# Computing the second layer's modulation beside the first routing stretch instead of beside the first mixer, in 1024-column blocks

## The chip, the cores and the metric

One NeuronCore of one Trainium2 chip runs the whole program in a single launch. The metric is device microseconds of one execution. Times shown are single executions and the median of three.

## The reference, cut to what matters

One inference step of a backbone with two layers, for 128 context tokens (the prompt) and 512 latent tokens (the sample), width 1024. Each layer has a modulated norm, a mixer (attention and retention in layer 0, differential and windowed attention in layer 1), a second modulated norm and a channel mixer that picks, for each token and each of 8 heads, 16 out of 16384 single-neuron experts.

```python
for layer in range(DEPTH):                      # DEPTH = 2
    mod_p = jnp.split(jax.nn.silu(c_ctx)[None, :] @ mod_w[layer] + mod_b[layer], 6, axis=-1)
    mod_s = jnp.split(jax.nn.silu(c) @ mod_w[layer] + mod_b[layer], 6, axis=-1)
    hp = ada(xp, norm_mix[layer], mod_p[0], mod_p[1])
    hs = ada(xs, norm_mix[layer], mod_s[0], mod_s[1])
    ...                                         # mixers: out_p, out_s
    xp = xp + mod_p[2][:, None, :] * out_p
    xs = xs + mod_s[2][:, None, :] * out_s
    xp = xp + mod_p[5][:, None, :] * peer(ada(xp, norm_ffn[layer], mod_p[3], mod_p[4]), ...)
    xs = xs + mod_s[5][:, None, :] * peer(ada(xs, norm_ffn[layer], mod_s[3], mod_s[4]), ...)
```

The modulation of a layer depends only on `c`, `c_ctx` and the weights `mod_w[layer]` (1024 x 6144 floats, 25.2 MB). It doesn't depend on the tokens, so layer 1's can be computed at any time before layer 1's first norm.

## The kernel before

The program has three stretches for each layer, one after the other, each with its own PSUM banks and SBUF pool.

- **M0, M1 (mixer).** The sample's mixer is the main work: input projections, attention, retention, output projection. PSUM: two banks `mm`, two double banks `S`, one `tr`, one `acc`. In M0 the first layer's modulation (`mod`, lines 325 to 358) runs first, at the same time as the first projections.
- **W0, W1 (routing).** `route` projects the queries of the channel mixer (`peer_q`, 16 steps, each loads a 512 KB weight block, splits it into a high and a low part with ScalarE and VectorE, L467 and L468, and multiplies, L478), finds each token's top experts (`pairs`), and then builds gate matrices (`gate_build`): VectorE makes one-hot rows, TensorE multiplies them into banks `gb` (L1403, L1404), ScalarE copies these to a tile `gst` (L1407) that goes to DRAM (`Gd`). Beside it run `dense_pre`, the first half of the dense expert product (`a_block`: load a 512 KB block `u`, split it with L1422 on ScalarE and L1423 on VectorE, 24 matmuls on L1434, a result `gpre` that goes to DRAM as `Ad`), and the gather. PSUM: three banks `mm`, four `gb`.
- **D0, D1 (dense).** The second half of the dense expert product. The prompt's mixer of layer 1, which needs layer 1's modulation, starts in D0.

The gather (`gather_tile`) fetches rows of expert weights by index, 128 x 1024 floats each: GpSimd issues an indirect DMA (L1323), VectorE multiplies (L1336) or accumulates (L1340). It runs through M0 to D1.

The order of the work is written out by generators. A `Task` steps a generator; `weave(main, *tasks)` steps the main one and gives every other task the main task's step cost times its rate as credit. Each engine executes its instructions in the order that results, and so does the DMA queue of SyncE (SP), on which all weight loads stand: a load that waits for a free tile holds up every load behind it.

The second layer's modulation is `mod_strips(1)` (from L361), a side task of M0 with rate `M1R` = 0.4. It goes over 12 strips of 512 columns. For each strip it takes an `mm` bank, loads eight 256 KB tiles `mw` (L371) through a ring of three (`MWB`), and for each tile does four matmuls (L373), one for each group of 32 PE columns; float32 operands make each of these two records in the trace. ScalarE copies the bank to `modsb` (L376), TensorE transposes it (L322) into an `mm` bank, and VectorE adds the bias (L381). 12 strips of 8 tiles are 96 tile steps.

In W0 the weight blocks of `peer_q` and the `u` blocks share one ring of three SBUF tiles, `w32` (`bufs=self.wb`, L461 and L1415): the load of a block waits until the block three before it has been split.

## Time and profile before

| | |
|---|---|
| median of 3 runs | 4050.77 us (4027.24 to 4058.07) |
| the profiled execution | 4050.72 us |
| its span, first to last instruction | 4048.9 us |
| outside the span | 1.8 us |
| M0, as far as the matmuls of `mod_strips` reach into it | 141.6 to 625.7 us |
| start of the chain's wait for the first `peer_q` block, in W0 | 716.95 us |
| first matmul of D0 | 1310.9 us |

Engines in the rows: PE is TensorE (PEld its weight loads), DVE VectorE, ACT ScalarE, POOL GpSimd, SP SyncE. "L373 PE MATMUL mm<-mw,c_silu" is line 373, a matmul that writes tile `mm` from `mw` and `c_silu`. In a wait, "A <- B: 15.3, 6, 5.8" says that A waited for B 15.3 us in all, 6 times, 5.8 us at the longest. The chain is the sequence of work that ended last, followed backwards from the last instruction; its shares are of the stretch named.

### The profile page before, as it was taken

The numbers are of one execution on the slowest core, as the hardware profiler recorded it, in microseconds if no ns is written. First come the engines' busy times: TensorE is split into PE (matmuls) and PEld (weight loads), VectorE is DVE, ScalarE is ACT, GpSimd is POOL, SyncE is SP. The second block draws the span as 40 slices with busy tenths as digits, with TensorE's granted clock in tenths as the row PEclk, the third lists the DMA queues.
The fourth block names the chain that finished last, engine by engine and source line by source line (L and its number), as shares of the span: only waits on it lengthen the run. The fifth ranks groups of instructions, "written<-read, shape, count | busy, mean of one in ns | idle before, by whom it ended". The sixth has DMA issues, their size and how long they took to land.

```text
span 4048.9 us, 57028 instructions
## 1 busy us (share of the span) xinstructions
PE 3653.0 (90%) x19986; PEld 3060.2 (76%) x19986; DVE 3180.2 (79%) x6370; ACT 1620.7 (40%) x2971; POOL 1621.2 (40%) x1138
## 2 busy tenths in 40 slices
PE   7888889889997999999998898988976999999998
PEld 3675556778886877888886676777875888888887
DVE  3238668999997767778897898899997667777777
ACT  3222223334776433433333333333476634333333
POOL 1004445320554234443464676532075233444342
PEclk9999989999998999999999999999997999999999
DMA  8556778775798889899896777777577889999886
GB/s 320 179 176 235 276 281 281 252 233 181 277 363 323 308 294 358 301 338 347 303 351 250 241 244 231 257 257 232 188 266 274 331 301 333 345 337 324 301 309 213
DMA packets 441087, 1134.86 MB, mean 280 GB/s; under 512 B 40640, under 2 KB 191360, under 8 KB 434528
## 3 DMA queue, kind: packets, MB, share of 16 engines
q0 software_dynamic: 147968, 537.36, 37.7%
q1 hardware_dynamic: 251408, 506.28, 36.3%
q10 hardware_dynamic: 41424, 87.57, 5.8%
q8 instruction: 157, 2.57, 0.2%
q14 instruction: 130, 1.06, 0.1%
HBM read 1045.08 MB, written 85.98 MB: 279 GB/s over the span
## 4 chain that ended last, share of the span: by engine, by line
PE 48%; DVE 16%; DMA 8%; issue 8%; ACT 5%; POOL 2%; ACTq 0%; DVEq 0%; POOLq 0%; SPq 0%
PE d L1457 21%; PE mm L1434 14%; PE mm L478 5%; DMA u<-ut 3%; DVE acc L1340 3%; DVE row L1336 2%; DMA row<-u,xi 2%; PE pm L482 2%; DVE ulo L1423 2%; ACT gst L1407 2%; POOL row L1323 1%; DMA Gd<-gst 1%; ACT uhi L1422 1%; PE S L708 1%; DMA Ad<-gpre 1%
## 5 line engine op out<-in xcount | busy, mean ns | idle before, releaser
L1323 POOL DMA_INDIRECT row<-v,xi x512 | 832.3, 1626 | 1114.1 <-DVE acc L1340 773.6
L1323 POOL DMA_INDIRECT row<-u,xi x512 | 681.3, 1331 | 789.0 <-DVE row L1336 585.2
L1434 PE MATMUL mm<-hhi,uhi 128*128 128x384 f32 x2048 | 709.6, 346 | 46.9 <-ACT uhi L1422 43.2
L1434 PE MATMUL mm<-hhi,ulo 128*128 128x384 f32 x2048 | 707.2, 346 | 49.3 <-DVE ulo L1423 49.1
L1434 PE MATMUL mm<-hlo,uhi 128*128 128x384 f32 x2048 | 702.6, 343 | 2.2 <-DVE hlo L452 1.6
L1336 DVE SCALAR_TENSOR_TENSOR row<-hn,row 128x1024 f32<-128x1024 f32 x512 | 630.0, 1257 | 47.4 <-DMA row<-u,xi 39.8
L1340 DVE SCALAR_TENSOR_TENSOR acc<-row,gw,acc 128x1024 f32<-128x1024 f32 x508 | 650.6, 1281 | 4.2 <-DMA row<-v,xi 1.6
L1457 PE MATMUL d<-vlo,Whi 128*128 128x512 f32 x1536 | 482.1, 394 | 5.6 <-DVE vlo L1498 5.6
L1457 PE MATMUL d<-vhi,Wlo 128*128 128x512 f32 x1536 | 479.0, 393 | 0.0
L1422 ACT CAST uhi<-u 128x1024 fp32r<-128x1024 f32 x256 | 268.8, 1050 | 491.8 <-PE mm L1434 226.8
L1423 DVE TENSOR_TENSOR ulo<-u,uhi 128x1024 fp32r<-128x1024 f32 x256 | 313.5, 1225 | 185.0 <-ACT uhi L1422 183.7
L1457 PE MATMUL d<-vhi,Whi 128*128 128x512 f32 x1536 | 437.3, 397 | 16.9 <-ACT vhi L1497 13.2
L1434 PEld LDWEIGHTS mm<-hhi,uhi 128*128 128x128 f32 x2048 | 396.5, 194 | 65.1 <-ACT uhi L1422 54.4
L1434 PEld LDWEIGHTS mm<-hhi,ulo 128*128 128x128 f32 x2048 | 395.3, 193 | 66.0 <-DVE ulo L1423 62.7
L1434 PEld LDWEIGHTS mm<-hlo,uhi 128*128 128x128 f32 x2048 | 395.2, 193 | 8.7 <-DVE hlo L452 2.0
L1457 PEld LDWEIGHTS d<-vhi,Whi 128*128 128x128 f32 x1536 | 288.1, 190 | 74.9 <-ACT vhi L1497 17.3
L1457 PEld LDWEIGHTS d<-vhi,Wlo 128*128 128x128 f32 x1536 | 288.0, 188 | 61.4 <-issue 0.2
L1457 PEld LDWEIGHTS d<-vlo,Whi 128*128 128x128 f32 x1536 | 286.4, 189 | 62.8 <-DVE vlo L1498 8.0
L1498 DVE TENSOR_TENSOR vlo<-v,vhi 128x1024 fp32r<-128x1024 f32 x256 | 312.2, 1221 | 14.2 <-ACT vhi L1497 13.9
L1505 ACT CAST Whi<-W 128x384 fp32r<-128x384 f32 x256 | 131.2, 513 | 433.1 <-PE d L1457 337.1
L1497 ACT CAST vhi<-v 128x1024 fp32r<-128x1024 f32 x256 | 268.5, 1051 | 53.3 <-DMA v<-v 41.9
L478 PE MATMUL mm<-hhi,whi 128*128 128x512 f32 x624 | 255.4, 410 | 31.5 <-DVE rvs L594 12.6
(470 smaller groups left out, 5776.4 us busy)
## 6 DMA issues: line engine op xcount, KB each, us to landing
u<-ut SPq DMA_DIRECT2D x256, 512.0 KB, 5.3
v<-v SPq DMA_DIRECT2D x256, 512.0 KB, 6.2
Gd<-gst ACTq DMA_DIRECT2D x48, 1024.0 KB, 8.7
G<-Gd SPq DMA_DIRECT2D x64, 768.0 KB, 8.8
w<-win SPq DMA_DIRECT2D x80, 512.0 KB, 4.7
w<-wq SPq DMA_DIRECT2D x64, 512.0 KB, 5.2
Ad<-gpre ACTq DMA_DIRECT2D x152, 192.0 KB, 4.5
pre<-Ad SPq DMA_DIRECT2D x152, 192.0 KB, 6.0
```

What stands on the lines that cost most here:

```text
L478: nc.tensor.matmul(ps[:, :st.T], wp[a][:, k], h[b][:, k], start=(n == 0), stop=(n == 23))
L482: nc.tensor.matmul(ps[:, :st.T], w32[:, k], h[:, k], start=(k == 0), stop=(k == 7))
L1323: nc.gpsimd.indirect_dma_start(out=r, out_offset=None, in_=self.A[f"{'uv'[n // 128]}{l}"], in_offset=bass.IndirectOffsetOnAxis(ap=xi[:, s: ...
L1336: nc.vector.scalar_tensor_tensor(r, hn, 1.0, r, op0=ALU.mult, op1=ALU.mult, accum_out=a[:, s:s + 1])
L1340: nc.vector.scalar_tensor_tensor(acc, r, w[:, s:s + 1], acc, op0=ALU.mult, op1=ALU.add)
L1422: nc.scalar.copy(hi, u)
L1423: nc.vector.tensor_tensor(lo, u, hi, op=ALU.subtract)
L1434: nc.tensor.matmul(ps[:, :ND], u[a][:, k], h[b][:, k, :ND], start=n == 0, stop=n == 23)
L1457: nc.tensor.matmul(acc[t][hf], a[:, ts], b[:, hf * 512:(hf + 1) * 512], start=(i == 0 and n == 0), stop=(i == 127 and n == 2))
L1497: nc.scalar.copy(vhi, v)
L1498: nc.vector.tensor_tensor(vlo, v, vhi, op=ALU.subtract)
L1505: nc.scalar.copy(whi, w)
```

## The change

`mod_strips` goes, and `mod_ahead` takes its place: a side task of W0 in layer 0, with rate 0.16. It goes over 6 blocks of 1024 columns; each tile `mw` is 128 x 1024 floats, 512 KB, and comes through the ring `w32`; each of its four matmuls has 256 columns. It has one PSUM bank of its own, `ms`, for the sums and the transposes, and W0 of layer 0 has three banks `gb` instead of four. M0 loses the task, its pool and its ring.

```diff
-M1R = 0.4
+M1R = 0.16
...
-    def mod_strips(self, l):
+    def mod_ahead(self, l):
...
-        for g in range(12):
-            ps = self.bank("mm")
+        for g in range(6):
+            ps = self.bank("ms")
             for k in range(8):
-                w = self.wk.tile([128, 512], F32, tag="mw", name="mw", bufs=MWB)
-                nc.sync.dma_start(w, self.A["mod_w"][l, k * 128:(k + 1) * 128, g * 512:(g + 1) * 512])
+                w = self.wk.tile([128, 1024], F32, tag="w32", name="mw", bufs=self.wb)
+                nc.sync.dma_start(w, self.A["mod_w"][l, k * 128:(k + 1) * 128, g * 1024:(g + 1) * 1024])
                 for j in range(4):
-                    nc.tensor.matmul(ps[32 * j:32 * j + 32, :128], c["silu"][:, k], w[:, j * 128:(j + 1) * 128],
+                    nc.tensor.matmul(ps[32 * j:32 * j + 32, :256], c["silu"][:, k], w[:, j * 256:(j + 1) * 256],
                                      start=(k == 0), stop=(k == 7), tile_position=(0, 32 * j))
-            sb = self.wk.tile([128, 128], F32, tag="sb", name="modsb", bufs=1)
-            nc.scalar.copy(sb, ps[:, :128])
-            yield 6.8
-            pt = self.bank("mm")
-            self.transpose(pt[:, :128], sb)
+                yield 1.0
+            sb = self.wk.tile([128, 256], F32, tag="msb", name="modsb", bufs=1)
+            nc.scalar.copy(sb, ps[:, :256])
+            pt = self.bank("ms")
+            for b in range(2):
+                self.transpose(pt[:, b * 128:(b + 1) * 128], sb[:, b * 128:(b + 1) * 128])
             for s in range(2):
...
-                if l == 0:
-                    weave(sample, prompt, ahead, gath)
-                    ahead.drain()
-                    ma.close()
-                else:
-                    weave(sample, prompt, gath)
+                weave(sample, prompt, gath)
...
-            with self.psum(f"W{l}", mm=W_MM, gb=W_GB), self.sbuf(f"W{l}"):
+            with self.psum(f"W{l}", mm=W_MM, gb=W_GB - 1, ms=1) if l == 0 else self.psum(f"W{l}", mm=W_MM, gb=W_GB), \
+                    self.sbuf(f"W{l}"):
...
                 side = [gath, pre]
+                if l == 0:
+                    side.append(Task(self, self.mod_ahead(1), M1R))
...
                 weave(route, *side, prompt)
```

Three places show what the change does to the order of instructions. Line numbers of the changed kernel differ by one or two. The first is SP's queue of loads in M0, in retention of the first head pair (`win` is the projection weight, `qf` and `qb` ramps). Before:

```order
L799 DMA ramp<-qf 128x512
L462 DMA w_3264<-win 128x1024
L371 DMA mw<-mod_w 128x512 x6
L799 DMA ramp<-qb 128x512
L462 DMA w_3311<-win 128x1024
L371 DMA mw<-mod_w 128x512 x2
L462 DMA w_3824<-win 128x1024
```

Now:

```order
L800 DMA ramp<-qf 128x512
L463 DMA w_2933<-win 128x1024
L800 DMA ramp<-qb 128x512
L463 DMA w_2980<-win 128x1024
L463 DMA w_3383<-win 128x1024
```

The loads of `mod_w` between the mixer's loads are gone, and nothing else in the queue has changed place. The second is the same queue where W0 begins (`wout` is the end of M0, `wq` the weight of `peer_q`, `ut` the blocks `u`). Before:

```order
L462 DMA w_5409<-wout 128x1024
L1416 DMA u_5557<-ut 128x1024
L462 DMA w_5594<-wq 128x1024
L1416 DMA u_5639<-ut 128x1024
L462 DMA w_5672<-wq 128x1024
L462 DMA w_5744<-wq 128x1024
L462 DMA w_5813<-wq 128x1024
L1416 DMA u_5886<-ut 128x1024
```

Now:

```order
L463 DMA w_4740<-wout 128x1024
L1417 DMA u_4887<-ut 128x1024
L370 DMA mw<-mod_w 128x1024 x2
L463 DMA w_4939<-wq 128x1024
L1417 DMA u_4984<-ut 128x1024
L370 DMA mw<-mod_w 128x1024
L463 DMA w_5023<-wq 128x1024
L370 DMA mw<-mod_w 128x1024
L463 DMA w_5101<-wq 128x1024
```

A load of `mod_w` now stands before nearly every load of `wq`, and two stand before the first; 24 of the 48 stand ahead of the first gate matrix, and 24 among the `u` loads of `gate_build`, there after every first or second `u`; the last fifteen `u` loads of W0 follow the last of them. The third is VectorE at a bias addition, before in M0 (a strip late in retention):

```order
L1336 SCALAR_TENSOR_TENSOR row,ga<-hn,row 128x1024
L381 TENSOR_TENSOR mod_854<-mm,c_mod_b 128x4 x2
L1336 SCALAR_TENSOR_TENSOR row,ga<-hn,row 128x1024
L386 SCALAR_TENSOR_TENSOR gs_855<-mod_854,c_gffn 128x8 x2
L819 TENSOR_TENSOR SD<-S,D_4426 128x512
```

and now in W0, in `peer_q` (the first of six):

```order
L1136 MATCH_REPLACE psr<-ptv,psc 128x128
L1138 MAX_INDEX pti<-ptv,psc 128x8
L381 TENSOR_TENSOR mod_4920<-ms,c_mod_b 128x8 x2
L469 TENSOR_TENSOR wlo<-w_5547,whi 128x1024
L1140 MAX ptv<-psr 128x8 x4
L1142 MAX_INDEX pti<-ptv,psr 128x8 x4
```

The two additions, which need a transpose on TensorE, stood among the gather's multiplications and now stand ahead of the split of a `peer_q` weight block and of the search for the top 16.

## Rows read from the trace of the kernel before

**Rows 1.** The page's head and its busy times of the engines.
```profile
span 4048.9 us, 57028 instructions
PE 3653.0 (90%) x19986; PEld 3060.2 (76%) x19986; DVE 3180.2 (79%) x6370; ACT 1620.7 (40%) x2971; POOL 1621.2 (40%) x1138
```

**Rows 2.** Busy time by stretch: start:end, length, engines, clock, DMA share, GB/s.
```profile
20.00:47.00 27.00, 20.41 (x95) 5.11 (x88) 11.30 (x41) 10.09 (x21) 0.00 (x0) 0.81 1.03 401
130.00:660.00 530.00, 463.50 (x3018) 323.69 (x3017) 327.29 (x834) 151.58 (x347) 182.31 (x154) 0.93 0.69 236
717.00:1050.00 333.00, 295.20 (x1585) 267.06 (x1586) 325.63 (x1061) 135.01 (x213) 84.05 (x62) 0.95 0.67 222
1050.00:1310.00 260.00, 219.41 (x1616) 207.66 (x1615) 220.26 (x308) 184.66 (x421) 133.84 (x66) 0.91 0.89 330
```

**Rows 3.** Groups of `mod_strips`, 130 to 660: busy, mean ns, idle before, releasers.
```profile
L373 PE MATMUL mm<-mw,c_silu 128*32 128x128 f32 x768 | 35.3, 288 | 8.8 <-DMA mw<-mod_w 7.9 <-ACT rqs L662 0.4 <-DVE xp L896 0.3
L322 PE MATMUL mm<-c_ident,modsb 128*128 128x128 f32 x12 | 3.8, 320 | 0.8 <-ACT modsb L376 0.8
L381 DVE TENSOR_TENSOR mod<-mm,c_mod_b 128x4 f32<-128x4 f32 x24 | 2.8, 158 | 15.3 <-PE mm L322 15.3
```

**Rows 4.** Busy time by stretch of line 373 alone: PE, PEld, clock, DMA.
```profile
516.00:660.00 144.00, 9.62 (x208) 4.52 (x208) 0.92 0.79 273
```

**Rows 5.** Chain of waits by line, 516 to 660.
```profile
by line: PE S L816 11.2%; PE mm L478 10.6%; issue 10.5%; PE acc L820 10.4%; PE S L708 8.0%; PE acc L781 7.3%; PE tr L756 7.1%; DMA row<-u,xi 4.9%; PE mm L756 4.3%; DVE row L1336 3.2%; PE mm L373 3.1%; PE acc L804 2.4%; PE mm L498 2.2%; POOL
```

**Rows 6.** Timeline, start and length: wide tile steps of layer 0, a narrow one.
```profile
47.89 1.91 PE L339 MATMUL tr<-modw,c_silu 128*32 128x512 f32 x12
...
549.24 0.42 PE L373 MATMUL mm<-mw,c_silu 128*32 128x128 f32 x8
549.60 1.12 PE L816 MATMUL S<-rqs,rks 128*128 128x512 f32 x2
```

**Rows 7.** Waits 130 to 660: line, for whom, us, times, longest.
```profile
DVE mod L381 <- PE mm L322: 15.3, 6, 5.8
...
PE mm L478 <- DVE rvs L594: 12.6, 3, 6.0
```

**Rows 8.** Waits of VectorE, 717 to 1050, the longest two.
```profile
DVE wlo L468 <- ACT whi L467: 3.6, 2, 3.3
DVE ada_t L445 <- PE mm L410: 1.3, 1, 1.3
```

**Rows 9.** Chain in order of time, W0: pieces of one a_block, of DMA.
```profile
716.95 7.10 DMA w<-wq
...
841.31 4.20 PE mm L1434 x24
...
1077.85 11.69 DMA Gd<-gst
1109.52 14.46 DMA Ad<-gpre
```

**Rows 10.** Chain by line, 1050 to 1310.
```profile
by line: PE mm L1434 25.6%; ACT gst L1407 15.4%; DMA Gd<-gst 10.4%; DMA Ad<-gpre 9.8%; issue 7.0%; ACT gjl L1397 5.6%; ACT uhi L1422 5.3%; DVE acc L1340 3.7%; PE gb L1403 2.3%; PE gb L1404 2.1%; ACT gpre L1436 2.0%; PE mm L1243 1.8%; DVE ul
```

**Rows 11.** DMA issues 1050 to 1310: count, KB, median us to landing.
```profile
u<-ut SPq DMA_DIRECT2D x34, 512.0 KB, 6.2
```

**Rows 12.** Splits of a u block, from the page: busy, mean ns, idle before.
```profile
L1422 ACT CAST uhi<-u 128x1024 fp32r<-128x1024 f32 x256 | 268.8, 1050 | 491.8 <-PE mm L1434 226.8
L1423 DVE TENSOR_TENSOR ulo<-u,uhi 128x1024 fp32r<-128x1024 f32 x256 | 313.5, 1225 | 185.0 <-ACT uhi L1422 183.7
```

**Rows 13.** Waits of TensorE for a gb bank: W0 (660 to 1310).
```profile
PE gb L1403 <- ACT gst L1407: 1.6, 4, 0.6
```

**Rows 14.** The same wait in W1 (3000 to 3260), also with four banks.
```profile
PE gb L1403 <- ACT gst L1407: 22.2, 7, 10.4
```

**Rows 15.** Tile d, the sums of the dense stretches: durations, first and last start.
```profile
L1457 PE MATMUL d<-vhi,Whi x1536: 387/389/792, 1310.9 to 4031.6; 128*128 128x512 f32 x192
```

More of the change, by code (lines that the diff above doesn't have):

```diff
@@ L60 @@
 ML = 1
-MWB = 3
 PDR = 0.7
@@ L366, in mod_strips @@
         self.mg[l] = m, gs
-        for g in range(12):
-            ps = self.bank("mm")
+        for g in range(6):
+            ps = self.bank("ms")
             for k in range(8):
-                w = self.wk.tile([128, 512], F32, tag="mw", name="mw", bufs=MWB)
-                nc.sync.dma_start(w, self.A["mod_w"][l, k * 128:(k + 1) * 128, g * 512:(g + 1) * 512])
+                w = self.wk.tile([128, 1024], F32, tag="w32", name="mw", bufs=self.wb)
+                nc.sync.dma_start(w, self.A["mod_w"][l, k * 128:(k + 1) * 128, g * 1024:(g + 1) * 1024])
                 for j in range(4):
-                    nc.tensor.matmul(ps[32 * j:32 * j + 32, :128], c["silu"][:, k], w[:, j * 128:(j + 1) * 128],
+                    nc.tensor.matmul(ps[32 * j:32 * j + 32, :256], c["silu"][:, k], w[:, j * 256:(j + 1) * 256],
                                      start=(k == 0), stop=(k == 7), tile_position=(0, 32 * j))
-            sb = self.wk.tile([128, 128], F32, tag="sb", name="modsb", bufs=1)
-            nc.scalar.copy(sb, ps[:, :128])
-            yield 6.8
-            pt = self.bank("mm")
-            self.transpose(pt[:, :128], sb)
+                yield 1.0
[4 more added lines that the diff above has]
+                self.transpose(pt[:, b * 128:(b + 1) * 128], sb[:, b * 128:(b + 1) * 128])
             for s in range(2):
-                nc.vector.tensor_tensor(m[:, 4 * g:4 * g + 4, s], pt[:, :128].rearrange("p (j r) -> p j r", r=32)[:, :, s],
-                                        c["mod_b"][:, l, 4 * g:4 * g + 4], op=ALU.add)
-            yield 0.5
+                nc.vector.tensor_tensor(
+                    m[:, g * 8:(g + 1) * 8, s].rearrange("p (j b) -> p j b", b=2),
+                    pt[:, :256].rearrange("p (b j r) -> p j b r", b=2, r=32)[:, :, :, s],
+                    c["mod_b"][:, l, g * 8:(g + 1) * 8].rearrange("p (j b) -> p j b", b=2), op=ALU.add)
         for i, (gain, o) in enumerate((("gmix", 8), ("gffn", 32))):
@@ L1640, in run @@
                 if l == 0:
-                    ma, mp = ExitStack(), ExitStack()
-                    pool = ma.enter_context(tc.tile_pool(name="mod1", bufs=1, reuse_waits="tile"))
-                    ahead = Task(self, self.mod_strips(1), M1R)
-                    ahead.ctx = (pool, pool, 6)
+                    mp = ExitStack()
                     pool = mp.enter_context(tc.tile_pool(name="mod0", bufs=1, side="right", reuse_waits="tile"))
```

## The prediction

> **What bounds the kernel now.** I read the page's head first, then busy time by stretch, then the waits and the chain inside the stretches that the change touches. Over the whole span TensorE is busy 90% and VectorE 79% [rows 1], but that mean says nothing on where a tile step costs time, so the stretches come next. In M0, from the first matmul of the strips to the end (130 to 660 us), TensorE is busy 463.50 of 530 us, VectorE 327.29, the DMA engines 0.69 of the time [rows 2]: nothing is full there, TensorE comes nearest. In the first part of W0 (717 to 1050 us, `peer_q` and `pairs`) VectorE is busy 325.63 of 333 us and TensorE 295.20: VectorE is full. Its longest wait there is 3.6 us in all [rows 8]. In the second part (1050 to 1310, `gate_build`) no engine is full, but the DMA engines are busy 0.89 of the time at 330 GB/s [rows 2], and on the chain stand 10.4% waits for `Gd` and 9.8% for `Ad` [rows 10]; single ones are 11.69 and 14.46 us long [rows 9]. So the work leaves a stretch with some room on every engine and enters one that is full on VectorE in its first part and nearly full on DMA in its second. Everything after W0 keeps its order, and I leave D0 to D1 as they are.
>
> **What M0 gives back.** The matmuls of the strips take 35.3 us of TensorE, the transposes 3.8 us, and TensorE waited 7.9 us for the `mw` loads [rows 3]. How much of it was on the path? From 516 to 660 us the chain spends 3.1% of 144 us on L373, which is 4.5 us, while L373 was busy 9.62 us there [rows 4, 5]: 46%. Going by TensorE's busy share in M0, 463.50 / 530, it would be 87%. I take the middle, 67%: 0.67 x (35.3 + 3.8) = 26 us for the work and 0.67 x 7.9 = 5 us for the waits. Three of the old tiles (3 x 0.26 MB) were loaded ahead of the first layer's modulation, where the DMA engines were full at 401 GB/s [rows 2]: 2 us. Sum: 33 us. Lower bound: 0.46 x 35.3 = 16 us. Upper bound: all of it, plus all 15.3 us that VectorE stood at the bias addition behind a transpose with the gather queued behind it [rows 3, 7]: 35.3 + 3.8 + 7.9 + 15.3 + 2 = 64 us. The upper end is not far-fetched, since each strip also held one of the two `mm` banks while its eight tiles came in; TensorE's 12.6 us of waiting for `rvs`, a copy out of an `mm` bank [rows 7], are the kind of wait that may shrink.
>
> **What W0 takes on**: seven terms, and a price that two of them use.
>
> (1) Start. Two 512 KB tiles now stand ahead of the first `wq` block, for which the chain already waits 7.10 us [rows 9]. 1.05 MB at 330 GB/s is 3 us.
>
> (2) A tile step's price. The trace has no 256-column step. A 128-column step (8 records) occupies TensorE 0.36 us, from 549.24 to the next start at 549.60; 512-column records came 12 in 1.91 us, so 8 in 1.27 us [rows 6]. On the straight line between, 256 columns take 0.66 us; the bounds are 0.36 and 1.27. 48 steps are 32 us, which is about what the 96 narrow ones took: TensorE's work is moved, not saved. 24 of the steps fall before 1050 us, 24 behind it. The Trainium skill (TensorEngine Tiling (Array Packing), section Tiling Modes) says that changing the tiling mode drains the engine; if that drain were the whole price, a step would stay at 0.36 us and the 48 would cost 17 us. Rows 6 speak for a price that grows with the columns, so the sum stays with 0.66.
>
> (3) TensorE, 717 to 1050. 24 x 0.66 + 1.9 us of transposes = 18 us, in a stretch with 333 - 295.20 = 38 us of idle TensorE under a full VectorE. I charge a quarter, 4.5 us (bounds 0 and 18). What hides it is VectorE's work; if TensorE gets late with a score matmul, VectorE waits at once.
>
> (4) VectorE at the bias addition. In M0 the twelve strips cost it 15.3 us of standing, 1.3 us for one [rows 3]. Three of the six new additions stand in the part where VectorE is full, ahead of a weight split on which TensorE depends: 3 x 1.3 = 4 us. Bounds 0 and 3 x 5.8 = 17 us, by the longest such wait [rows 7].
>
> (5) The ring. A `u` or `wq` block whose slot was last held by an `mw` tile can only be requested when TensorE has done that tile's matmuls, where before it was requested when VectorE had split the block three earlier. From request to use it then takes 6.2 us of loading [rows 11] and 1.05 + 1.23 us of splitting [rows 12], 8.5 us. Between lie one or two blocks of 24 matmuls at 4.20 us [rows 9] and, in `gate_build`, the gate matmuls; the 34 `u` loads of 260 us [rows 11] make 7.6 us to a block. With two blocks between, nothing is late; with one, about 1 us, in some 10 places, and half as much again in `peer_q`: 5 us. Bounds 0 and 25.
>
> (6) TensorE, 1050 to 1310. 24 x 0.66 + 1.9 = 18 us. TensorE is busy 219.41 of 260 us [rows 2] but stands on only a third of the chain (25.6 + 2.3 + 2.1 + 1.8% [rows 10]). I take half, 9 us (bounds 6 and 18).
>
> (7) DMA, 1050 to 1310. 24 x 0.524 MB = 12.6 MB. If the engines were full they would need 38 us more at 330 GB/s. The stretch moves 86 MB, so the load rises by 15%, and the 20.2% of the chain that are DMA waits [rows 10], 53 us, would rise to match by 8 us if waits grew only as the bytes do. At a share of 0.89 they grow faster: 15 us, bounds 0 and 38. On this the Trainium skill (DMA: Bandwidth & Descriptors, section Specifications) is harsher: it gives about 358 GB/s as one core's limit from HBM, and by it 12.6 MB in a stretch that runs near it are 35 us. The trace shows 401 GB/s from 20 to 47 us [rows 2], so I don't take that figure as a wall.
>
> (8) The fourth `gb` bank. In W0 TensorE waited 1.6 us for ScalarE to empty one [rows 13]; in W1, the same code with the same four banks, 22.2 us [rows 14]. So the margin is thin. With three: 8 us, bounds 0 and 22. Behind a gate matmul that waits stand the 24 matmuls of the next a_block, and behind these the DMA of `Ad`.
>
> Sum of W0: 3 + 4.5 + 4 + 5 + 9 + 15 + 8 = 48.5 us. Net: 48.5 - 33 = +15.5 us on the execution's own 4050.7 us (span 4048.9 and 1.8 outside), 4066 us. That execution equals the median of the runs shown, so nothing is corrected. The prompt's mixer of layer 1 starts in D0 and finds its modulation finished, since the last `mw` load stands before the last 15 `u` loads of W0.
>
> **Rivals.**
>
> A. M0 was held up by the strips more than by their matmuls: the blocked `mm` bank and the VectorE waits go as well, and M0 returns 64 us. W0 hides nearly all: 3 us of start, 6 of TensorE, 8 of DMA, 3 of the rest, 20 us. Net -44 us: 4007 us. For it: the 15.3 us on VectorE and the gather bursts behind them. Against it: the chain holds only 46% of the strips' matmuls, so other waits lie close beneath.
>
> B. A wash. As forecast, but the ring and the bank cost nothing and the DMA waits grow only as the bytes do: 48.5 - 5 - 8 - 7 = 28.5 against 33 us, 4046 us. For it: 1.6 us of bank waits in W0. Against it: the same wait in W1.
>
> C. Slower, through DMA in `gate_build`: `Gd`, `Ad`, the gather and the `u` loads already fill 0.89 of the engines; the new tiles come on top in full, ScalarE stands longer at `gst`, three banks fill sooner, and `u` loads land late so that the ring's lateness counts. It decides where the share passes about 0.97 for the whole stretch. 38 (DMA) + 22 (banks) + 15 (ring) + 18 (TensorE) + 11.5 (start, terms 3 and 4) = 104 us, less 33: +71 us, 4122 us. The skill's figure on HBM would have it so. For it: 20.2% of the chain; against it: VectorE's and ScalarE's share of the same chain, under which some of it hides.
>
> That the change doesn't do what it says is out: the order of the instructions shows the loads gone from M0 and all 48 in W0.
>
> **How the numbers follow.** The forecast, with errors of its own of about 25 us either way, gets 0.45, B 0.20, C 0.20, A 0.15. A measurement of this kernel can tell about 1%, 40.5 us, from no change: the bounds are 4010 and 4091 us. Faster by over 1%: 0.12 from A and 0.01 from B, 0.13. Slower: 0.20 from C and 0.10 from the forecast's upper end, 0.30. Within 1%: 0.57. The range has to take in most of C and A's edge: 4010 to 4118 us. The likeliest case's own range is 4041 to 4091.
>
> **What would show it.** M0 should end 16 to 64 us earlier: the wait for the first `peer_q` block, now at 716.95 us, should begin near 684. From there to the first matmul of D0, now at 1310.9 [rows 15], was 594 us and should be about 642. In 717 to 1050 VectorE should stay above 95% with new waits of a few us at the bias additions; in `gate_build` the waits for `Gd` and `Ad` should grow and waits of L1403 for `gst` appear. The D stretches and M1, W1 should keep their length within 10 us. The forecast is wrong if W0 grows by less than 30 us (towards A or B) or more than 75 (C), or if the difference lies behind W0 at all.

## The result and the profile after

The changed kernel takes 4025.0 us (median of 19 runs, 4014.5 to 4033.8), the kernel before on the same chips 4049.7 us (19 runs, 4027.2 to 4065.4). The ratio is 0.9943 with a 95% interval of 0.9931 to 0.9955: 0.57% faster, 24.7 us, where 15.5 us slower was forecast. That is less than the 1% that the prediction took for the least difference one can tell, but it is clear, and its sign is the other one.

The head of the page after, beside [rows 1]:

```profile
span 4020.8 us, 56136 instructions
PE 3640.4 (91%) x19602; PEld 3033.4 (75%) x19602; DVE 3182.0 (79%) x6358; ACT 1618.8 (40%) x2965; POOL 1588.2 (40%) x1138
```

The stage ends below are read off the first starts of certain instructions, in us. M0 ends with the first matmul that spreads the sample's norm in W0. The first part of W0 ends at the first copy to `gst`, the gate part at the first matmul of `d`, and so on. The second line is a repeat of the kernel before.

```
                 M0 ends  W0 first  W0 gate  W0 sum  d starts   D0    M1    W1    D1    end
before             717.9     290.4    302.6   593.0    1310.9  890.0 441.3 624.9 781.8 4048.9
before, again      707.2     291.0    303.0   594.0    1301.3  890.1 447.6 622.2 781.7 4042.9
changed            657.7     294.9    331.6   626.5    1284.1  896.1 444.2 622.6 773.7 4020.8
difference         -60.2      +4.5    +29.0   +33.5     -26.8   +6.1  +2.9  -2.3  -8.1  -28.1
```

M0 gave back 60 us by these two profiles and W0 took 33.5. What lies behind W0 sums to -1.4 us. M0's end scatters: the two profiles of the kernel before differ by 10.7 us there, and four later kernels whose M0 is the changed one's end it at 649.6 to 653.0. So the gain of M0 is 50 to 68 us, while W0 and its two parts repeat within 1 us. A third profile with the M0 of the kernel before (run 14 below) ends it at 707.7. The 717.9 is thus the odd one of three, and 50 to 58 us is the likelier part of that range. The start of `d`, beside [rows 15]:

```profile
L1458 PE MATMUL d<-vhi,Whi x1536: 387/389/774, 1284.1 to 4003.5; 128*128 128x512 f32 x192
```

Busy time by these stretches, in the columns of [rows 2] (engines PE, PEld, DVE, ACT, POOL, then granted clock, DMA share, GB/s), the kernel before:

```profile
120.00:718.00 598.00, 525.65 (x3290) 370.76 (x3291) 375.20 (x899) 171.23 (x377) 218.35 (x180) 0.93 0.70 241
718.00:1008.00 290.00, 258.13 (x1327) 233.10 (x1328) 283.04 (x1003) 104.13 (x145) 63.49 (x56) 0.95 0.66 218
1008.00:1311.00 303.00, 257.40 (x1880) 242.50 (x1880) 263.26 (x364) 216.13 (x489) 153.42 (x72) 0.92 0.87 318
```

And the changed one:

```profile
120.00:658.00 538.00, 476.18 (x2510) 341.93 (x2510) 372.32 (x864) 165.94 (x358) 217.47 (x180) 0.94 0.65 220
658.00:953.00 295.00, 279.49 (x1575) 235.41 (x1575) 286.73 (x1016) 107.04 (x153) 66.05 (x56) 0.97 0.79 267
953.00:1284.00 331.00, 278.73 (x2026) 250.18 (x2025) 260.60 (x365) 214.25 (x486) 129.29 (x72) 0.91 0.87 317
```

In M0 TensorE is busy 49.5 us less and idle 10.5 us less (598 - 525.65 = 72.4, 538 - 476.18 = 61.8). Of the 49.5, 39.1 us are the strips' matmuls and transposes [rows 3]; the other 10.4 are the mixer's own matmuls, at a granted clock of 0.94 in place of 0.93 (the mean of a stretch over TensorE's two levels, 2.4 and 1.2 GHz). Against the repeat, where TensorE is busy 517.8 us in M0 at 0.94, these are only 3 us. So M0 gave back as much as the strips' TensorE time and, in this profile, 11 to 21 us more. One wait went that the prediction had named: TensorE's 12.6 us for `rvs` [rows 7] are 12.1 and 12.4 in the other two profiles of this M0, and in the changed kernel there are none, nor the 7.9 us for `mw`. A new wait takes up part of it:

```profile
PE acc L821 <- DVE SD L820: 9.1, 2, 4.6
```

In the first part of W0 TensorE takes on 21 us and the stretch grows by 4.5: TensorE's idle time falls from 31.9 to 15.5 us. VectorE stays at 97%. In the gate part TensorE takes on 21 us, and the stretch grows by 29. The DMA share there is 0.87 before and after, at 318 and 317 GB/s.

The new task alone (tile `ms`: steps, transposes, additions, copies), in the same two stretches:

```profile
658.00:953.00 295.00, 24.24 (x240) 6.31 (x240) 0.66 (x6) 1.10 (x3) 0.97 0.79 267
953.00:1284.00 331.00, 15.33 (x156) 4.09 (x156) 0.72 (x6) 1.15 (x3) 0.91 0.87 317
```

Without the 6 transposes in each, that is 29 of the 48 tile steps in the first part and 19 in the second. Their group in all of W0, in the columns of [rows 3], and one step in the timeline (start, length):

```profile
L372 PE MATMUL ms<-mw,c_silu 128*32 128x256 f32 x384 | 36.7, 411 | 6.5 <-DMA mw<-mod_w 6.5
```

```profile
704.85 0.64 PE L372 MATMUL ms<-mw,c_silu 128*32 128x256 f32 x8
705.42 1.16 PE L1127 MATMUL mm<-sk,pq 128*128 128x128 f32 x8
```

TensorE's longest waits in the gate part (line, for whom, us, times, longest):

```profile
PE gb L1404 <- ACT gst L1408: 18.2, 15, 4.4
PE pm L398 <- ACT sq L396: 10.1, 1, 10.1
PE mm L1435 <- ACT uhi L1423: 9.4, 8, 2.2
PE ms L372 <- DMA mw<-mod_w: 4.2, 2, 3.5
```

The wait for a `gb` bank, 1.6 us before [rows 13] and 8.8 in the repeat of the kernel before, is 18.2 us now. The longest waits of VectorE in the first part hold none at the new additions:

```profile
DVE ulo L1424 <- PE mm L1127: 3.0, 1, 3.0
DVE ada_t L446 <- PE mm L411: 2.2, 1, 2.2
DVE ptv L1134 <- ACT psc L1129: 2.0, 2, 1.1
DVE wlo L469 <- ACT whi L468: 0.7, 2, 0.5
```

### The profile page after: what moved, and what is told of

Same layout as the page of the kernel before. It is cut to its first block, busy times and chain, and to the rows that moved or that the text cites. A ratio compares the mean times of both kernels' runs of the same rounds, so it can differ in the third digit from the quotient of the medians.

```text
span 4020.8 us, 56136 instructions
## 1 busy us (share of the span) xinstructions
PE 3640.4 (91%) x19602; PEld 3033.4 (75%) x19602; DVE 3182.0 (79%) x6358; ACT 1618.8 (40%) x2965; POOL 1588.2 (40%) x1138
## 4 chain that ended last, share of the span: by engine, by line
PE 34%; DVE 12%; DMA 9%; issue 8%; ACT 3%; POOL 2%; ACTq 0%; DVEq 0%; SPq 0%; POOLq 0%
PE d L1458 17%; PE mm L1435 10%; DMA u<-ut 5%; DVE row L1337 2%; DMA row<-u,xi 2%; PE mm L479 2%; DVE acc L1341 2%; PE pm L483 2%; POOL row L1324 2%; DVE vlo L1499 1%; DVE ulo L1424 1%; DMA v<-v 1%; ACT uhi L1423 1%; PE S L709 1%; DVE wlo L469 1%
## 5 line engine op out<-in xcount | busy, mean ns | idle before, releaser
L1324 POOL DMA_INDIRECT row<-v,xi x512 | 801.4, 1565 | 1151.1 <-DVE acc L1341 841.3
L1337 DVE SCALAR_TENSOR_TENSOR row<-hn,row 128x1024 f32<-128x1024 f32 x512 | 626.7, 1250 | 58.4 <-DMA row<-u,xi 48.5
L1423 ACT CAST uhi<-u 128x1024 fp32r<-128x1024 f32 x256 | 268.7, 1050 | 485.2 <-PE mm L1435 209.5
L1498 ACT CAST vhi<-v 128x1024 fp32r<-128x1024 f32 x256 | 268.5, 1050 | 62.2 <-DMA v<-v 46.1
```

The costliest lines, as they stand in the source:

```text
L1324: nc.gpsimd.indirect_dma_start(out=r, out_offset=None, in_=self.A[f"{'uv'[n // 128]}{l}"], in_offset=bass.IndirectOffsetOnAxis(ap=xi[:, s: ...
L1337: nc.vector.scalar_tensor_tensor(r, hn, 1.0, r, op0=ALU.mult, op1=ALU.mult, accum_out=a[:, s:s + 1])
L1423: nc.scalar.copy(hi, u)
L1498: nc.scalar.copy(vhi, v)
```

## The experiments

Two questions were open. Why did M0 return 60 us, when 33 were forecast? And which of W0's terms were real? The theories on M0 were these: the strips' own work on TensorE; their loads, for their traffic and for the ring, behind which SP's queue stands; the held `mm` bank; VectorE at the additions. The ends of M0 are compared with both profiles of the kernel before, 707.2 and 717.9, so each difference has two ends; the end by 707.2 is the likelier one. Runs 1 to 8 and run 12 are one execution each.

One thing limits all of them. The section on the kernel before says that each engine executes its instructions in the order that the generators give. That is not all: the kernel is built with `schedule_with_timeline_sim=True`, and in the traces the order is another one. A strip's eight steps, which the generator hands over in one piece, stand in the kernel before in 58 pieces among the mixer's matmuls. And an edit of the strips changes the order of the rest with them. Of the 2897 matmul records outside the strips up to M0's end, all but two stand at the same place in the sequence in the three profiles of this M0. In the changed kernel 822 stand elsewhere, by up to 66 places; in runs 1 to 7 it is 318 to 842. What this is worth shows in W0, where runs 1 to 7 edit nothing: 1609 to 1962 of its 3205 records stand elsewhere, 24 to 57 of them have crossed from the gate part into the first, and the gate part takes 292 to 297 us in place of 303, the whole of W0 586 to 592 in place of 593 to 594. So a difference of that size, some 10 us in one of W0's parts, can't be given to the edit itself.

**1. The strips without their loads.**

```diff
-                w = self.wk.tile([128, 512], F32, tag="mw", name="mw", bufs=MWB)
-                nc.sync.dma_start(w, self.A["mod_w"][l, k * 128:(k + 1) * 128, g * 512:(g + 1) * 512])
+                if g == k == 0:
+                    w = self.wk.tile([128, 512], F32, tag="mw", name="mw", bufs=MWB)
+                    nc.sync.dma_start(w, self.A["mod_w"][l, :128, :512])
```

> The kernel before, with the strips' 96 loads replaced by one tile loaded once; all their matmuls, transposes and additions stay (the modulation of layer 1 is computed from wrong weights). Marker: the first matmul that spreads the sample's norm in W0, 717.9 us before, 657.7 us in the changed kernel, 60 us earlier. Theory W (the steps' occupancy of TensorE is what M0 gave back): only the 7.9 us of load waits go, marker 6 to 12 us earlier. Rival L (the 25 MB of loads: their waits, and the mm bank held while a strip's eight tiles come in): marker 30 us earlier or more.

Measured: 4000.3 us (before, on the same chip, 4050.6); M0 ends at 671.9, 35 to 46 us earlier. Its stretch of M0, and the group of the strips:

```profile
120.00:672.00 552.00, 495.03 (x3290) 360.31 (x3290) 370.70 (x892) 168.62 (x371) 226.02 (x180) 0.97 0.63 214
```

```profile
L374 PE MATMUL mm<-mw,c_silu 128*32 128x128 f32 x768 | 23.9, 274 | 2.5 <-DVE mod L382 1.8 <-DVE xp L897 0.3 <-ACT rqs L663 0.3
```

The loads matter far more than the 7.9 us of waits for them [rows 3] say. Not all is waiting: TensorE is busy 30.6 us less with the same 3290 matmuls, 11.4 of it in the strips, the rest in the mixer at a granted clock of 0.97 in place of 0.93 (against the repeat, at 0.94, it is 23 us less in all). The 11.4 are no waits either: without loads a strip's steps stand together, in 14 pieces in place of 58, such as this one of eight steps:

```profile
140.59 1.95 PE L374 MATMUL mm<-mw,c_silu 128*32 128x128 f32 x64
142.48 0.72 PE L490 MATMUL mm<-c_sel,sq 128*128 128x2 f32 x5
```

**2. The loads without most of the matmuls** (of eight steps, the last alone).

```diff
-                for j in range(4):
+                for j in range(4 if k == 7 else 0):
...
-                                     start=(k == 0), stop=(k == 7), tile_position=(0, 32 * j))
+                                     start=True, stop=True, tile_position=(0, 32 * j))
```

> The kernel before, with the matmuls of seven in eight tile steps left out (only the last tile of a strip is multiplied, so the modulation of layer 1 is wrong); all 96 loads, the transposes and the additions stay, and the mm bank is taken only when the last step begins. Theory W: 7/8 of the occupancy goes, marker 35 to 50 us earlier than 717.9. Rival L, by its loads: marker 0 to 12 us earlier. Rival L, by the held bank: 30 us or more, like W; the run with the first and last step tells these two apart.

Measured: 4006.4 us; M0 ends at 670.0, 37 to 48 earlier. The strips' group is 5.4 us, 29.9 less. So M0 is shorter by 7 to 18 us more than that. TensorE's idle time, 67.5 us, is near the repeat's 69.4, so the rest isn't TensorE's waits for the ring; against the repeat 6 us of it are the mixer's own matmuls.

**3. The same with the first and the last step,** so that the `mm` bank is held as long as before.

```diff
-                for j in range(4):
+                for j in range(4 if k in (0, 7) else 0):
```

> As the run with the loads only, but the first and the last tile step of each strip are multiplied, so that the mm bank is held over all eight loads again (modulation of layer 1 wrong). Theory W: 6/8 of the occupancy goes, marker 30 to 45 us earlier than 717.9, at most 8 us later than with the last step alone. Rival H (the held bank): most of the gain of the loads-only run is lost, marker within 15 us of 717.9.

Measured: 4011.5 us; M0 ends at 677.3, 30 to 41 earlier; the group is 9.4 us, 25.9 less. Against run 2 M0 is 7 us longer, with 4 us more of matmuls, so the held bank itself costs some 3 us, less than M0's scatter. As a main cause it falls.

**4. No transposes and no additions.**

```diff
+        nc.vector.memset(m, 0.0)
...
-            yield 6.8
-            pt = self.bank("mm")
-            self.transpose(pt[:, :128], sb)
-            for s in range(2):
-                nc.vector.tensor_tensor(m[:, 4 * g:4 * g + 4, s], pt[:, :128].rearrange("p (j r) -> p j r", r=32)[:, :, s],
-                                        c["mod_b"][:, l, 4 * g:4 * g + 4], op=ALU.add)
-            yield 0.5
+            yield 7.3
```

> The kernel before, without the strips' transposes and bias additions (modulation of layer 1 left at zero); loads, tile steps and copies stay. Theory W: 3.8 us of transposes go, marker 3 to 6 us earlier than 717.9. Rival V (VectorE standing at the additions, 15.3 us, with the gather behind it): marker 12 to 25 us earlier.

Measured: 4016.7 us; M0 ends at 693.3, 14 to 25 earlier. The 3.8 us of transposes and the 15.3 us that VectorE stood [rows 3] make 19.1. TensorE's busy time is that of the repeat (519.4 and 517.8 us); its idle time is 53.9 us in place of 69 to 73, and its waits for `rvs`, 12.6 us before [rows 7], have nearly gone:

```profile
PE mm L473 <- DVE rvs L589: 1.7, 3, 0.8
```

The copy to `rvs` is VectorE's, and in the kernel before it came late behind a standing addition: VectorE stood 4.1 us for a strip's transpose up to 499.0, worked off the gather's rows and weight splits that stood behind it, and began this copy at 515.6, with TensorE waiting 6.0 us. So the standing was on the path, by about its own length; the second bank that a strip takes for the transpose went as well, and its part isn't separated.

**5. The first seven steps reduced to one matmul of two columns,** so that TensorE still comes by for each tile.

```diff
+                if k < 7:
+                    nc.tensor.matmul(ps[:32, :2], c["silu"][:, k], w[:, :2], start=True, stop=True, tile_position=(0, 0))
-                for j in range(4):
+                for j in range(4 if k == 7 else 0):
...
-                                     start=(k == 0), stop=(k == 7), tile_position=(0, 32 * j))
+                                     start=True, stop=True, tile_position=(0, 32 * j))
```

> The kernel before, where the first seven tile steps of a strip do one matmul of two columns in one column group instead of four of 128 (modulation of layer 1 wrong). Every load still waits for TensorE to release its ring slot, the bank is held over the eight loads, transposes and additions stay; of TensorE's time for the steps a quarter or less is left. Marker as in the runs before (717.9 us before, 670.0 with loads only). Theory W (occupancy): marker 30 to 50 us earlier than before. Rival Q (SP's queue stands at loads that wait for TensorE, and the mixer's loads behind them; TensorE stands at loads): marker within 20 us of before.

Measured: 4030.9 us (before on that chip 4044.1); M0 ends at 700.1, 7 to 18 earlier. The strips:

```profile
L373 PE MATMUL mm<-mw,c_silu 128*32 128x2 f32 x168 | 14.4, 180 | 13.3 <-DMA mw<-mod_w 10.8 <-PE mm L322 1.2 <-DVE mod L384 0.6
L376 PE MATMUL mm<-mw,c_silu 128*32 128x128 f32 x96 | 5.6, 307 | 0.0
```

TensorE's time in them falls by 15.3 us, from 35.3 to 20.0, and M0 by 7 to 18. The end moved by less than 20 us, which was to speak for rival Q, but the rows don't bear it out. Run 2 ends 30 us earlier, and of these 30 only 6 are TensorE's idle time, in which its waits for the ring and for late loads would stand; 14.6 are the strips' own time, and the rest is the mixer's matmuls at a granted clock of 0.94 in place of 0.92. Against the repeat the strips' 15 us less are offset by 4 us more of the mixer's matmuls and 4 us more of idle time; VectorE stood 20.1 us at the additions in place of 15.3. A step of two columns takes TensorE 0.15 us here, from 406.56 to the next start at 406.71, and one of 128 columns 0.36 [rows 6]:

```profile
406.56 0.22 PE L373 MATMUL mm<-mw,c_silu 128*32 128x2 f32 x2
406.71 0.50 PE L481 MATMUL mm<-hhi,whi 128*128 128x512 f32 x1
```

And steps that follow one another are cheaper: one takes 0.36 us, two take 0.57 (538.72 to 539.29 in the kernel before), eight take 1.89 (run 1's lines above). By the straight line through these a step costs 0.22 us and a visit of TensorE to the strips some 0.14 beside it.

**6. The loads stay, but nobody reads them;** the steps read one fixed tile.

```diff
+                if g == k == 0:
+                    w0 = self.wk.tile([128, 512], F32, tag="mw0", name="mw0", bufs=1)
+                    nc.sync.dma_start(w0, self.A["mod_w"][l, :128, :512])
...
-                    nc.tensor.matmul(ps[32 * j:32 * j + 32, :128], c["silu"][:, k], w[:, j * 128:(j + 1) * 128],
+                    nc.tensor.matmul(ps[32 * j:32 * j + 32, :128], c["silu"][:, k], w0[:, j * 128:(j + 1) * 128],
```

> The kernel before, with all 96 loads issued through their ring of three but read by nobody; the tile steps read one more tile that was loaded once (modulation of layer 1 wrong). TensorE's work, the transposes and additions, and the 25 MB of traffic stay; what goes is that TensorE waits for a load and that a load waits for TensorE. Without the loads the marker stood at 671.9. Rival Q: marker near that, 30 us or more earlier than 717.9. Rival T (the traffic itself slows the gather and the mixer's loads): marker within 15 us of 717.9. Theory W: 6 to 12 us earlier.

Measured: 4038.8 us; M0 ends at 697.1, 10 to 21 earlier. Its row of M0 beside that of run 1:

```profile
120.00:697.00 577.00, 506.27 (x3305) 367.38 (x3305) 378.06 (x912) 173.58 (x383) 226.70 (x180) 0.95 0.70 240
```

Runs 1 and 6 do the same steps, in the same 14 pieces; 25 us lie between them. That is what the loads cost by themselves, with no reader to hold their ring (96 x 0.262 = 25 MB, a DMA share of 0.70 in place of 0.63): 11 us of it in TensorE's busy time at 0.95 in place of 0.97 and 14 in idle time. The two ran on different chips, and some of their order differs, so the 25 are good to 10 us or so. Beside the repeat of the kernel before, run 6's M0 is shorter by 10 us, as its strips are: with no reader and no wait for a load, TensorE is idle 70.8 us, as before. That speaks against rival Q.

**7. The new form in the old place:** six blocks of 1024 columns in M0, two tiles in the ring.

```diff
-MWB = 3
+MWB = 2
-        for g in range(12):
+        for g in range(6):
...
-                w = self.wk.tile([128, 512], F32, tag="mw", name="mw", bufs=MWB)
+                w = self.wk.tile([128, 1024], F32, tag="mw", name="mw", bufs=MWB)
...
-            sb = self.wk.tile([128, 128], F32, tag="sb", name="modsb", bufs=1)
-            nc.scalar.copy(sb, ps[:, :128])
-            yield 6.8
+            sb = self.wk.tile([128, 1024], F32, tag="mw", name="modsb", bufs=MWB)[:, :256]
+            nc.scalar.copy(sb, ps[:, :256])
+            yield 13.6
...
```

> The kernel before with six blocks of 1024 columns in M0 (256-column matmuls, 48 steps, a ring of two 512 KB tiles, results right): half the visits of TensorE to the strips, half the groups of transposes and additions. If each visit costs beyond its columns: marker 8 to 25 us earlier than 717.9. If the columns and bytes are the price: within 6 us.

Measured: 4014.4 us in one run; M0 ends at 688.2, 19 to 30 earlier, W0 is 586.9. The strips take 30.3 us of TensorE, and VectorE stands 5.5 us at the additions in place of 15.3. `modsb` has one of the ring's two tiles here.

**8. The kernel before, once more.**

> The kernel before, unchanged, for the scatter of the markers from one profiled execution to the next. Marker at 717.9 within 6 us, W0 593 within 6 us, if the stretches repeat as well as the totals do.

Measured: 4044.7 us, M0 707.2: the first profile's M0 was 10.7 us longer, more than expected. TensorE is busy 517.8 us in it in place of 525.7. W0, 594.0, repeats.

**9. Run 7 timed.** No further edit.

> The wide blocks in M0 again (48 tile steps, a ring of two tiles), now timed; one look gave a marker at 688 and W0 at 587. Theory X (most of the gain of the changed kernel is in the number of visits and loads, not in the place): ratio to the kernel before 0.992 to 0.996, level with the changed kernel's 0.994. Theory Y (the place: M0 has no room, W0 has): ratio 0.997 to 1.001, clearly above the changed kernel's.

Measured: 4026.2 us, ratio 0.9942 (0.9926 to 0.9958): as much as the change itself. Half as many strips, and a third of the standing at additions, give with the work left in M0 as much as the change gets by moving it. Of the 22 us M0 has 18 to 29 by its profile (it ends at 689.1); W0, which was not edited and has another order, has 6 to 7.

**10. Four `gb` banks beside `ms`** in the changed kernel (the eighth bank was unused).

```diff
-            with self.psum(f"W{l}", mm=W_MM, gb=W_GB - 1, ms=1) if l == 0 else self.psum(f"W{l}", mm=W_MM, gb=W_GB), \
+            with self.psum(f"W{l}", mm=W_MM, gb=W_GB, ms=1) if l == 0 else self.psum(f"W{l}", mm=W_MM, gb=W_GB), \
```

> The changed kernel with four gb banks in W0 of layer 0 again, beside the bank ms: 3 + 4 + 1 = 8 banks, one bank of the eight was unused. Marker: from the norm's matmul at the start of W0 to the first matmul of D0, 593 us in the kernel before, 626.4 in the changed one. Theory P (the bank: TensorE waited 18.2 us for gst in the gate stretch, 1.6 before): W0 12 to 18 us shorter than in the changed kernel, the whole 10 to 18 us faster. Rival D (DMA and TensorE work hold the stretch): W0 0 to 4 us shorter.

Measured: 4020.7 us, ratio 0.9923 (0.9900 to 0.9945). The gate part is 320.9 in place of 331.6, and the wait is down from 18.2 us:

```profile
PE gb L1404 <- ACT gst L1408: 4.0, 7, 1.1
```

10.7 us lie between the two expectations. It is not all of the gate part's 29, and another order moves the gate part by as much (runs 1 to 7). The interval of the ratio overlaps the change's, so that the whole is faster isn't shown.

**11. Rate 0.3,** so that all strips fall in the first part.

```diff
-M1R = 0.16
+M1R = 0.3
```

> The changed kernel with rate 0.3 in place of 0.16, so that nearly all tile steps stand in the part of W0 that VectorE fills (before the first gst copy) and few or none among the gate matrices. In the changed kernel that part took 294.9 us against 290.4, the gate part 331.5 against 302.6. If the steps, their loads or their ring cost the gate part something: gate part 8 to 20 us shorter, first part at most 6 us longer. If the gate part grew through the bank alone: gate part within 4 us, first part the same or longer.

Measured: 4018.1 us, ratio 0.9918 (0.9899 to 0.9936). The last step starts at 957.9. The gate part is 310.4 (-21), but the first part 317.7 (+23), which was not expected. Its longest wait of VectorE and of SP's queue:

```profile
DVE wlo L469 <- ACT whi L468: 19.9, 7, 6.3
```

```profile
SPq L370 <- PE ms L372: 50.6, 16, 8.9
```

SP stands at the next `mw` load until TensorE has read an older tile, the `wq` blocks behind it come late, and VectorE, full in this part, stands 19.9 us at their split. At 0.16 that wait is 0.7 us. W0 as a whole is 628.1 us, no shorter than the change's 626.5.

**12. The changed kernel without the 48 loads.**

```diff
-                w = self.wk.tile([128, 1024], F32, tag="w32", name="mw", bufs=self.wb)
-                nc.sync.dma_start(w, self.A["mod_w"][l, k * 128:(k + 1) * 128, g * 1024:(g + 1) * 1024])
+                if g == k == 0:
+                    w = self.wk.tile([128, 256], F32, tag="mw", name="mw", bufs=1)
+                    nc.sync.dma_start(w, self.A["mod_w"][l, :128, :256])
...
-                    nc.tensor.matmul(ps[32 * j:32 * j + 32, :256], c["silu"][:, k], w[:, j * 256:(j + 1) * 256],
+                    nc.tensor.matmul(ps[32 * j:32 * j + 32, :256], c["silu"][:, k], w,
```

> The changed kernel with one small tile loaded once in place of the 48 loads (modulation of layer 1 wrong); all matmuls, transposes, additions and banks stay, and the ring w32 serves u and wq blocks alone. W0 was 626.4 us in the changed kernel. Theory P: 0 to 6 us shorter. Rival D (12.6 MB more in the gate part, and the ring): 15 us shorter or more.

Measured: 3997.7 us in one run; W0 605.4, 21 us shorter. The number is on the side of the loads, but the run says something else too. With no loads to wait for, the order comes out with every strip in the first part, at the same rate of 0.16. The new task in the two stretches, and the stretches whole:

```profile
653.00:947.00 294.00, 33.33 (x396) 13.95 (x396) 1.38 (x12) 2.20 (x6) 0.98 0.67 217
947.00:1258.00 311.00, 0.00 (x0) 0.00 (x0) 0.00 (x0) 0.00 (x0) 0.90 0.85 306
653.00:947.00 294.00, 284.95 (x1730) 241.99 (x1731) 283.71 (x1021) 107.57 (x155) 62.08 (x56) 0.98 0.67 217
947.00:1258.00 311.00, 261.46 (x1870) 243.64 (x1869) 261.87 (x360) 214.43 (x485) 142.09 (x72) 0.90 0.85 306
```

The first part hides 33.3 us of strips on TensorE: it takes 294.2 us, where the changed kernel's takes 294.9 and that of the kernel before 290.4. So it is not TensorE's time that made it 23 us longer in run 11 but the loads, and run 11's two rows speak for their ring. And its gate part holds no strip, only three banks: 311.2 us, as in run 11 (310.4).

**13. Four banks in W0, five in W1, rate 0.2** in the changed kernel.

```diff
-M1R = 0.16
+M1R = 0.2
-            with self.psum(f"W{l}", mm=W_MM, gb=W_GB - 1, ms=1) if l == 0 else self.psum(f"W{l}", mm=W_MM, gb=W_GB), \
+            with self.psum(f"W{l}", mm=W_MM, gb=W_GB, ms=1) if l == 0 else self.psum(f"W{l}", mm=W_MM, gb=W_GB + 1), \
```

> The changed kernel with four gb banks in W0 of layer 0, five in W1 (all eight PSUM banks in use in both), and rate 0.2, so that the steps end earlier in the gate stretch. Theory P: the gate part of W0 10 to 20 us shorter than the changed kernel's 331.6, W1 5 to 15 us shorter than its 622.6, the whole 15 to 30 us faster than the changed kernel, ratio to the kernel before 0.987 to 0.991. Rival: W1's waits for a bank lie beside DMA waits and give nothing, ratio as with four banks in W0 alone, 0.992.

Measured: 3999.5 us (3995.5 to 4003.6), ratio 0.9873 (0.9855 to 0.9890): the fastest of all versions that compute everything. Its gate part:

```profile
951.00:1260.00 309.00, 271.46 (x1987) 246.58 (x1984) 260.80 (x363) 215.39 (x485) 144.59 (x72) 0.95 0.89 328
```

W0 is 610.8 us, 15.7 shorter than the change's, 22 of it in the gate part against 6.3 lost in the first. W1 is 620.6: of the 5 to 15 us expected from a fifth bank there, 2 to 4 came.

**14. Five `gb` banks in the kernel before.**

```diff
-W_GB = 4
+W_GB = 5
```

> The kernel before, with five gb banks in W0 and W1 in place of four, so that all eight PSUM banks are used there; the strips stay in M0. Theory P: W0 shorter by 2 to 8 us (its waits for a bank were 1.6 us) and W1 by 5 to 15 (22.2 us), ratio 0.995 to 0.998. Rival: other waits lie close beneath, ratio 0.998 to 1.001.

Measured: 4050.9 us, ratio 1.0004 (0.9990 to 1.0019). Nothing. The wait for a bank in W1, 22.2 us [rows 14], is halved, but the wait for `gjh`, 17.3 us before, takes its place:

```profile
PE gb L1403 <- DVE gjh L1394: 29.5, 12, 7.8
...
PE gb L1403 <- ACT gst L1407: 10.6, 3, 5.5
```

**15. The wide strips in M0 with five banks** (the edits of runs 7 and 14 together).

> Both together: wide blocks in M0 and five gb banks in W0 and W1. If the two effects add: ratio 0.987 to 0.993, level with the best run so far (0.9873: moved to W0, four and five banks, rate 0.2). If the work is better placed in W0: above 0.993.

Measured: 4028.3 us, ratio 0.9942 (0.9925 to 0.9959), the same as run 9.

## Why the prediction was wrong

**M0, the step that failed.** "How much of it was on the path?" was answered with 46% from the chain, 87% from TensorE's share, and "I take the middle, 67%". M0 gave back 50 to 68 us in place of 33, and 60 by the first two profiles, near the upper bound of 64. M0's length is TensorE's busy time and its idle time, so each run can be split up (us, from 120 to M0's end; "other matmuls" is the rest of the busy time, transposes among it):

```
run                          M0      strips   other matmuls   idle
before                      597.9     35.3       490.3        72.3
before, again               587.2     34.8       483.0        69.4
the same M0, in run 14      587.6     35.2       479.9        72.5
1 no loads                  551.9     23.9       471.1        56.9
2 last step alone           550.0      5.4       477.1        67.5
3 first and last step       557.3      9.4       478.3        69.6
4 no additions              573.3     38.0       481.4        53.9
5 two columns               580.1     19.6       487.2        73.3
6 nobody reads the loads    577.1     25.3       481.0        70.8
7 wide blocks               568.2     30.3       476.7        61.3
the change                  537.7      0.0       475.9        61.8
```

In runs 2, 3, 5 and 6 the idle time stays where it was, 67.5 to 73.3 us. Together they have 79.5 us less of strips than the repeat and 84.3 us less of M0, singly 7 for 15 up to 37 for 29. So the share of the strips' own time was about all of it, not two thirds: some 39 us, not 26. No run holds the order of the rest fixed, so this rests on the agreement of the sizes. The chain's 3.1% in 516 to 660 [rows 5] misled me, for a chain follows one route back: a wait of TensorE for `rvs` goes to VectorE there, though VectorE was late behind a strip (run 4). The step failed a second time in what it left beside that time. VectorE's standing at the additions, 15.3 us, was held for the upper bound only, and in run 4, without it, TensorE's idle time is 15 to 19 us shorter. The loads were charged 5 + 2 us, and by run 1 against run 6 they cost about 25. The parts overlap: 39.1, 25 and 15.3 sum to 79, and 50 to 68 came back. How much of the 11 to 29 us beyond TensorE's own 39 belongs to traffic, to VectorE and to the new order of the mixer's instructions stays open, for M0's scatter of 10 us and the worth of order are as large.

**W0, 48.5 forecast, 33.5 measured.** The sum was too high by a third, mostly in the first part:

- (1), (3), (4), and the ring of (5) in `peer_q`, some 14 us: +4.5. The new work's TensorE time there, 24 us with 29 steps in place of the 24 forecast, is hidden but for this (run 12 hides 33.3). The three additions cost nothing: no such wait stands among VectorE's. At rate 0.16 the ring costs nothing visible, though at 0.3 it costs about 20 us (run 11): the mechanism was right, and the rate decides.
- (2) 0.66 us a step: 0.57 from start to next start (704.85 to 705.42), or 0.76 as the group's busy time over 48 steps (36.7 us): the forecast was near. The Trainium skill (TensorEngine Tiling (Array Packing), section Tiling Modes) has the change of mode drain the engine. As the whole price that would leave 0.36 us, so here it is not; what run 5's lines leave for a visit beside its columns is some 0.14 us.
- (8) 8 us for the fourth bank: 8 (310.4 and 311.2 with three banks and no strip in the gate part, against 302.6 and 303.0 with four). With the strips in it, run 10 has 10.7. The agreement may be luck: another order moves the gate part by 6 to 11 us with four banks throughout (runs 1 to 7), so the bank's price isn't known to better than that.
- (6) and (7), 9 + 15 us: the strips in the gate part cost 18 us with four banks (320.9 - 302.6) and 20 to 21 with three (331.6 - 311.2, or - 310.4). The sum was near, with the same reserve. Which of the two it is isn't separated. TensorE's busy time in the changed kernel is 17.3 us above run 12's, at the same three banks, which would be most of it, and the DMA share is 0.87 in place of run 12's 0.85. ScalarE's waits for `Gd` decide nothing: 8.2 us before and 7.3 after, but 26.4 in run 10 and 27.0 in run 12, with the strips there and without.

**The rivals.** A had M0 right (64 us) and W0 too low (20); B had W0 nearly right (28.5) and M0 as low as I had. C's bound, a DMA share of 0.97, was not come near. The truth lay between A and B, 4007 and 4046 us. I gave A 0.15 because "other waits lie close beneath" the strips. Two of them, for `rvs` and for `mw`, 20 us in all, went with the strips; 9 us came back at `SD`. The range of 4010 to 4118 us holds the measured 4025, but by its width alone: it was to take in A's edge, while the likeliest case's own range, 4041 to 4091, missed. Of the 40 us between forecast and result 17 to 35 lie in M0 and 15 in W0.

**What would show it.** M0 was to end 16 to 64 us earlier: it did, but 26 us before the 684 I named. W0 was to be about 642: 626.5. Waits for `gst` appeared as said; those for `Gd` did not grow, and no new wait came at the additions. D0 to D1 kept their lengths within 10 us.

## What to carry to other kernels

Side work that stands in the order of an engine which is busy nearly nine tenths of a stretch can cost that stretch all of its time, also where nothing is full and the chain names other lines. Charge it whole, and then add what its loads do to the traffic and what other engines stand for it. Work that goes into a stretch bound by another engine can be hidden there as long as its loads stay ahead of its readers, so try its rate before its place. Count the PSUM banks before one is taken from a consumer: here an unused one stood by, and with it, a fifth bank in W1 and another rate the gain went from 0.6% to 1.3%. And where the instructions are ordered anew when an edited kernel is built, compare the order of all the rest before a difference is put down to the edit: here W0, with no edit of its own, became 2 to 8 us shorter, and its gate part 6 to 11.

## What the runs showed beside that

- Without the loads of the strips, the same matmuls of M0 ran at a granted clock of 0.97 (run 1) in place of 0.93 to 0.95 in the three profiles of M0 before, and took 9 to 19 us less outside the strips. Why the clock was higher there, no run here tells.
- M0 of one and the same program differed by 10.7 us between two profiles, 7.8 of it in TensorE's busy time, while W0 repeated within 1 us. A stretch needs its own scatter before a difference in it is read, and this is the scatter of one order only.
- A wait for a bank is worth very different things: 9 to 17 us more of it stood beside a gate part 8 to 11 us longer in W0, and 11 us less of it in W1 (20.0 to 9.0, run 13) moved that stretch by 2, with 14 us more of waits for `gjh`.
- The fastest version's gain is larger than those of its parts (0.9873; banks alone 0.9923). Beside the shorter W0 its mean granted clock over the span is 0.960 to 0.964 in its five executions, against 0.949 to 0.956 in nine of the kernel before beside them, and D0 is 14 us shorter than the changed kernel's; this was not taken apart.
